# Moving tile starts by small padding tiles, a subtraction from GpSimd to VectorE, and a sixth slot for split weights

## The chip, the cores and the metric

The kernel runs on one core of a Trainium2 chip. The metric is the device time of one execution in microseconds (us); lower is better. TensorE (PE) multiplies, VectorE (DVE), ScalarE (ACT) and GpSimd (POOL) do the element work, and SyncE (SP) issues nearly all loads.

## The reference, cut to what matters

Two transformer blocks follow one another on 256 tokens of width 1024, all in float32. What matters here is where the large products are:

```python
# first block
proj  = rms_norm(x) @ w_in                  # attention, RWKV and memory mixers
x     = x + mixed @ w_out
for e in range(16):                         # mixture of experts, two experts of 16 for each token
    y += gate[:, e:e+1] * ((silu(xt @ w_gate[e]) * (xt @ w_up[e])) @ w_down[e])
x     = x + y
# second block, two layers
h = h + 0.5 * (silu(n(h) @ w1) * (n(h) @ w3)) @ w2     # swiglu, 1024 -> 2816 -> 1024
h = h + mixer(n(h))                                    # layer 0: dilated + top-k attention; layer 1: sliding window
h = h + 0.5 * (silu(n(h) @ w1) * (n(h) @ w3)) @ w2
```

So the second block is, in order: swiglu 0, the hybrid mixer (`hyb`), swiglu 1, swiglu 2, the sliding window mixer (`swa`), swiglu 3.

## The kernel before, in words

**Products in three parts.** A float32 product is made of three matmuls on the type float32r. Each operand is split into a rounded part and what is left (`xh`, `xl` for activations; `wh`, `wl` for weights), and `mm3` (lines 97 to 101) issues rounded x rounded, rounded x rest and rest x rounded into one PSUM bank. In the profile these are the three matmuls of lines 99, 100 and 101. The first operand of a matmul is the stationary one, of 128 columns, loaded by a weight load before it; the second is the moving one, of 256 or 512 columns.

- In `proj2`, `projN` and `project_back` a 128-column slice of the activations (`xh`/`xl`, `hh`/`hl`, `oh`/`ol`, `o`) is stationary, and 512 columns of weights move (256 for the last sixth of a swiglu's gate and up, for `swa_kv` and for `win_m`).
- In `projT` a 128-column slice of the weights is stationary and 256 columns of activations move.
- Parts of the experts' products are plain float32 (lines 1298 and 1324), with 64 stationary columns; they are no part of this.

The profile names a matmul by its operands as out<-moving,stationary: `acc<-wh,xh` has `xh` stationary.

**Splitting the weights.** Weights are loaded in 2 MB pieces into tiles `raw`, and `split` (lines 88 to 95) makes the two parts of 1024 columns at a time: ScalarE rounds (line 93, `wh`), VectorE subtracts (line 94, `wl`). The pair goes into one of five slots in turn, three of the pool `wsp` and two of `lend`, set by the cycle in `weights`. A slot is free again when the last matmul that reads it has run.

**Order.** Each engine's stream is ordered ahead of time by a scheduler that simulates a timeline (`schedule_with_timeline_sim=True`); each engine is then given its stream in that order. So any edit can change the order of neighbours.

**The experts' gather.** In `moe`, `hx` and `hy` are the two parts of the residual `h`. ScalarE rounds (`hx`), GpSimd subtracts (`hy`, line 1171). `gather` (line 1189) multiplies them with 0/1 matrices `P`, which pick 64 tokens for each expert, and the experts follow.

**Where tiles start.** Each partition of the on-chip memory is filled from address 0: first the scratch of `dynamic_dma_scratch_size` bytes, then four constants of 32 bytes each, then the pools in the order in which they are opened, and in a pool one place for each tag and buffer in the order of first use. Sizes are rounded up to 32 bytes. Added up from the shapes, this gives these starts in bytes, and what is left after division by 128 and by 512:

| tile | start before | mod 128 | mod 512 |
|---|---|---|---|
| pool `const` (`ident`, `mhalf`, `cols`, `cm`, `L`, `over`, `flag`) | 1152 | 0 | 128 |
| pool `wk`: `h` | 4544 | 64 | 448 |
| `xh` (also `o` and `yr`) / `xl` (also `o` and `xe`) | 12736 / 20928 | 64 | 448 |
| `raw` (and `memT` in one) | 37760 | 0 | 384 |
| `wh`, `wl` of `wsp` and `lend` | 86912 to 123776 | 0 | 384 |
| experts: `hx`, `hy` and `P` | 162816 to 181248 | 0 | 0 |
| swiglu: `hh` / `hl` | 144256 / 166784 (swiglu 3: 148352 / 170880) | 0 | 384 |
| `hyb`: `oh` / `ol` | 160192 / 168384 | 64 | 448 |
| `swa`: `oh` / `ol` | 149376 / 157568 | 0 | 384 |

Slices of these tiles are 512, 1024 or 2048 bytes apart, so every slice has its tile's rest modulo 512.

Of the kernel before, what the change touches and what calls it, by code (L numbers as in the profile page):

```python
# [11 lines left out]
F32 = mybir.dt.float32  # L12
# [4 lines left out]
OP = mybir.AluOpType  # L17
# [9 lines left out]
class Net:  # L27
# [36 lines left out]
    def setup(self):  # L64
        nc = self.nc
        self.ident = self.const.tile([128, 128], F32, name="ident")
        nc.gpsimd.memset(self.ident, 1.0)
        nc.gpsimd.affine_select(self.ident, self.ident, pattern=[[-1, 128]], compare_op=OP.is_equal,
                                fill=0.0, base=0, channel_multiplier=1)
        self.mhalf = self.const.tile([128, 1], F32, name="mhalf")  # L70
        nc.gpsimd.memset(self.mhalf, -0.5)
        self.cols = self.const.tile([128, NCOL], F32, name="cols")
        nc.scalar.dma_start(self.cols, self.I["cols"])

    def col(self, name, i=0, n=1):
        o = COLS[name][0]
        return self.cols[:, o + i:o + i + n]
# [83 lines left out]
    @contextmanager  # L161
    def weights(self, extra, nsplit):

        with ExitStack() as st:
            pools = list(self.base)
            if extra:
                pools += [st.enter_context(self.tc.tile_pool(name=self.nm("raw"), bufs=extra))] * extra
            self.splits = itertools.cycle([self.wsp] * NW + [self.lend] * nsplit)
            self.ring = itertools.cycle(pools)
            yield  # L170
        self.ring = itertools.cycle(self.base)
# [260 lines left out]
    def hyb(self, h, x, follow):  # L432
        nc, wk = self.nc, self.ph
# [4 lines left out]
                                channel_multiplier=1)  # L438
        xh, xl, rs = x
        ps = self.projN(self.by_k(self.load(self.I["hyb_c"]), 296), 0, 296, xh, xl, True)  # L440
        cw = self.natural(ps, self.pair(264, "cw0", "cw1"), rs)
        kiT = self.repeated_T([z[:, 264:296] for z in ps], rs, "kiT", 1)
        bc = self.row_bc(rs)
        ch = wk.tile([128, 2, T], F32R, name="ch", tag="ch", bufs=1)
# [1 line left out]
        for t in range(2):  # L446
# [3 lines left out]
            ps = self.trp()  # L450
# [680 lines left out]
    def moe(self, h, x):  # L1131

        nc, wk = self.nc, self.ph
        mm, tr, tt = nc.tensor.matmul, nc.tensor.transpose, nc.vector.tensor_tensor
        cm = self.cm
        ck = lambda n: cm[:, COLSM[n][0]:COLSM[n][0] + COLSM[n][1]]
        st = lambda shape, tag, dt=F32: wk.tile([128] + shape, dt, name=self.nm(tag), tag=tag, bufs=1)
        bc = lambda z, *s: z.to_broadcast([128] + list(s))
        L, rs = x
# [7 lines left out]
        for i, op in enumerate((OP.is_ge, OP.is_gt)):  # L1147
# [11 lines left out]
        ps = self.trp()  # L1159
# [7 lines left out]
        hx, hy = ([wk.tile([128, D], F32R, name=self.nm(z), tag=f"{z}{t}", bufs=1) for t in range(2)]  # L1167
                  for z in ("hx", "hy"))
        for t in range(2):
            nc.scalar.copy(hx[t], h[t])  # L1170
            nc.gpsimd.tensor_tensor(hy[t], h[t], hx[t].bitcast(F32), OP.subtract)

        def places(q):

# [260 lines left out]
    def front(self, h):  # L1435

        nc = self.nc
        for t in range(2):
            nc.sync.dma_start(h[t], self.I["x"][t * 128:(t + 1) * 128])
        with ExitStack() as more:  # L1440
            with self.banks(acc=3, tr=2, rk=3), self.weights(0, 0):
                x = self.mixers(h, more, lambda: self.logits(h))
            self.ctx.enter_context(self.banks(acc=6, tr=2))
            with self.phase():
                y = self.moe(h, x)
        ahead = [self.load(self.I["ffn0"][0], 2)]
        self.moe_overflow(h)
        return y, ahead
# [25 lines left out]
NW = 3  # L1474
# [202 lines left out]

# [10 lines left out]
```

## Time and profile before

| | |
|---|---|
| median of 3 runs | 1452.94 us (1452.23 to 1453.97) |
| profiled execution | 1451.34 us, of which the span from first to last instruction is 1449.6 us |
| PE busy / VectorE / ScalarE / GpSimd | 1383.6 / 760.6 / 605.6 / 127.9 us |
| mean granted TensorE clock | 0.983 of 2.4 GHz |

A matmul's duration in the profile overlaps with the next one's, so the time that a matmul costs in a dense stretch is read as the distance between the starts of neighbours, called the pitch below. It is worked out from the first and the last start of a stretch and the number of steps between them.

### The profile page before, as it was taken

To read this page: it belongs to the slowest core of one execution; us is meant where nothing else is said; L and a number is where in the kernel's file an instruction comes from. 1 tells how busy PE (TensorE), PEld (TensorE's weight loads), DVE (VectorE), ACT (ScalarE), POOL (GpSimd) and SP (SyncE) were. 2 spreads that over 40 slices of the span, in tenths; PEclk is the share of its full clock that TensorE was granted. 3 is DMA by queue.
4 is the path that set the end of the run, shared out by engine and by line. 5 is a ranking of instruction groups with operands and counts; after the bars stand their busy time and mean duration, and the time that the engine had idled before them with its cause. 6 is when DMAs were issued, how large, how long until landed. Compare 5 with 4: busy or idle time off the path is not lost.

```text
span 1449.6 us, 18902 instructions
## 1 busy us (share of the span) xinstructions
PE 1383.6 (95%) x7650; PEld 1042.0 (72%) x7650; DVE 760.6 (52%) x1233; ACT 605.6 (42%) x951; POOL 127.9 (9%) x150
## 2 busy tenths in 40 slices
PE   7899989999998999999898999999999989999997
PEld 6687664344336888878677888878888877788886
DVE  6967651112125555456865555455555466555544
ACT  5345431111114444347454444344444456444442
POOL 6514110000001000010111000010000010100001
PEclk9999889999998999999999999999999999999999
DMA  7243379999965544355333544454444632365520
GB/s 305 90 183 139 145 319 368 419 409 419 420 285 213 194 174 175 130 216 194 126 117 139 210 174 174 153 225 175 175 174 160 240 129 111 131 214 182 185 88 29
DMA packets 35371, 293.81 MB, mean 203 GB/s; under 512 B 3728, under 2 KB 8112, under 8 KB 16080
## 3 DMA queue, kind: packets, MB, share of 16 engines
q1 hardware_dynamic: 29952, 286.58, 52.4%
q10 hardware_dynamic: 5328, 5.98, 1.2%
q8 instruction: 62, 1.02, 0.3%
q14 instruction: 29, 0.24, 0.0%
HBM read 291.45 MB, written 1.10 MB: 202 GB/s over the span
## 4 chain that ended last, share of the span: by engine, by line
PE 64%; DVE 2%; ACT 1%; POOL 1%; issue 1%; ACTq 0%; POOLq 0%; DVEq 0%
PE acc L101 20%; PE acc L99 20%; PE acc L100 19%; PE tr L206 1%; PE acc L322 1%; PE tr L318 1%; DVE wl L94 1%; POOL xl L135 1%; ACT wh L93 1%; PE acc L288 1%; PE acc L289 1%; PE acc L323 0%; ACT sq L113 0%; DVE h L371 0%; PE tr L127 0%
## 5 line engine op out<-in xcount | busy, mean ns | idle before, releaser
L94 DVE TENSOR_TENSOR wl<-raw,wh 128x1024 fp32r<-128x1024 f32 (+1 forms) x338 | 412.5, 1223 | 377.6 <-ACT wh L93 377.0
L93 ACT CAST wh<-raw 128x1024 fp32r<-128x1024 f32 (+1 forms) x349 | 363.4, 1045 | 412.8 <-PE acc L101 367.7
L101 PE MATMUL acc<-wh,xl 128*128 128x512 f32 (+2 forms) x896 | 336.0, 376 | 7.2 <-POOL xl L135 7.2
L99 PE MATMUL acc<-wh,xh 128*128 128x512 f32 (+2 forms) x896 | 337.2, 378 | 1.7 <-ACT xh L134 1.2
L100 PE MATMUL acc<-wl,xh 128*128 128x512 f32 (+2 forms) x896 | 335.2, 374 | 3.0 <-DVE wl L94 3.0
L101 PEld LDWEIGHTS acc<-wh,xl 128*128 128x128 f32 x896 | 169.5, 189 | 41.4 <-POOL xl L135 9.2
L100 PEld LDWEIGHTS acc<-wl,xh 128*128 128x128 f32 x896 | 169.8, 190 | 35.3 <-DVE wl L94 3.7
L99 PEld LDWEIGHTS acc<-wh,xh 128*128 128x128 f32 x896 | 169.8, 189 | 35.1 <-ACT xh L134 2.2
L101 PE MATMUL acc<-wh,hl 128*128 128x512 f32 x352 | 137.4, 390 | 0.0
L100 PE MATMUL acc<-wl,hh 128*128 128x512 f32 x352 | 137.2, 390 | 0.0
L99 PE MATMUL acc<-wh,hh 128*128 128x512 f32 x352 | 136.7, 389 | 0.0
L105 POOL TENSOR_SCALAR rstd<-ss 128x1 f32<-128x1 f32 x22 | 8.2, 371 | 940.8 <-ACT sq L113 938.9
L101 PEld LDWEIGHTS acc<-wh,hl 128*128 128x128 f32 x352 | 66.1, 188 | 13.6
L99 PEld LDWEIGHTS acc<-wh,hh 128*128 128x128 f32 x352 | 66.1, 188 | 13.6
L100 PEld LDWEIGHTS acc<-wl,hh 128*128 128x128 f32 x352 | 66.1, 188 | 13.5
L99 PE MATMUL acc<-xh,wh 128*128 128x256 f32 x224 | 65.8, 294 | 2.1 <-DVE cur L653 1.3
L100 PE MATMUL acc<-xl,wh 128*128 128x256 f32 x224 | 63.9, 286 | 1.8 <-POOL xl L135 1.0
L101 PE MATMUL acc<-xh,wl 128*128 128x256 f32 x224 | 64.2, 288 | 0.0
L1298 PE MATMUL acc<-half,xe 128*64 128x512 f32 x248 | 59.6, 596 | 0.0
L1331 DVE TENSOR_SCALAR yf<-tr,gate 128x512 f32<-128x512 f32 x16 | 12.0, 751 | 81.0 <-PE tr L1324 80.8
L99 PEld LDWEIGHTS acc<-xh,wh 128*128 128x128 f32 x224 | 43.4, 194 | 5.9 <-ACT wh L93 2.7
L100 PEld LDWEIGHTS acc<-xl,wh 128*128 128x128 f32 x224 | 43.1, 193 | 2.5 <-POOL xl L135 1.3
(458 smaller groups left out, 1748.7 us busy)
## 6 DMA issues: line engine op xcount, KB each, us to landing
raw<-in_ffn SPq DMA_DIRECT2D x63, 2048.0 KB, 8.0
half<-in_moe SPq DMA_DIRECT2D x45, 1024.0 KB, 12.9
raw<-in_moe SPq DMA_DIRECT2D x13, 2048.0 KB, 15.6
raw<-in_hyb SPq DMA_DIRECT2D x7, 2048.0 KB, 7.9
wl<-in_moe SPq DMA_DIRECT2D x23, 512.0 KB, 13.7
wh<-in_moe SPq DMA_DIRECT2D x23, 512.0 KB, 14.8
raw<-in_win SPq DMA_DIRECT2D x4, 2048.0 KB, 10.1
raw<-in_swa SPq DMA_DIRECT2D x4, 2048.0 KB, 8.7
```

What stands on the lines that cost most here:

```text
L93: nc.scalar.copy(hi[:, :n], x)
L94: self.lo.tensor_tensor(lo[:, :n], x, hi[:, :n].bitcast(F32), OP.subtract)
L99: mm(out, a[0], b[0], start=start, stop=False)
L100: mm(out, a[0], b[1], start=False, stop=False)
L101: mm(out, a[1], b[0], start=False, stop=stop)
L135: (nc.vector if a else nc.gpsimd).tensor_tensor(dl, xf, dh.bitcast(F32), OP.subtract)
L206: nc.tensor.transpose(ps[:, i * 128:(i + 1) * 128], m[:, i * 128:(i + 1) * 128], self.ident)
L288: nc.tensor.matmul(ps[:, 0:128], qT[r, 0:128], kT[r, 0:128], start=True, stop=True)
L289: nc.tensor.matmul(ps[:, 128:384], qT[r, 128:256], kT[r, :], start=True, stop=True)
L318: nc.tensor.transpose(pt[:, i * 128:(i + 1) * 128], s2[e][:, i * 128:(i + 1) * 128], self.ident)
L322: nc.tensor.matmul(po[r, :T], v[0][:, c:c + 64], pT[:, :T], start=True, stop=False)
L1298: last = mm(ps[c][e * 64:e * 64 + 64, :], xe[:, k, o + e * 64:o + e * 64 + 64], w[i][e][:, c * 512:c * 512 + 512], start=k == 0, stop=k == 7)
```

## The change

- `room` makes a tile of a given number of float32 words that nothing reads, and fills it with zeros on GpSimd. One of 16 words (64 bytes) goes into the pool `const` behind `mhalf`, one into the pool `wk` after the experts.
- The scratch shrinks from 1024 to 512 bytes.
- `cw0` and `cw1` of `hyb` take 320 words each where they took 264; the same 264 are used.
- `hy` is made on VectorE, in two halves of 512 columns for each of the two tiles, where GpSimd made each in one.
- Where `weights` is entered for the second block (`nsplit` is 2), the cycle of slots gets a sixth one in a pool of its own.

```diff
         nc.gpsimd.memset(self.mhalf, -0.5)
+        self.room(self.const, 16)
         self.cols = self.const.tile([128, NCOL], F32, name="cols")
...
+    def room(self, pool, words):
+
+        z = pool.tile([128, words], F32, name=self.nm("room"), tag=f"room{words}", bufs=1)
+        self.nc.gpsimd.memset(z, 0.0)
...
-            self.splits = itertools.cycle([self.wsp] * NW + [self.lend] * nsplit)
+            spare = [st.enter_context(self.tc.tile_pool(name=self.nm("spare"), bufs=1))] if nsplit else []
+            self.splits = itertools.cycle([self.wsp] * NW + [self.lend] * nsplit + spare)
...
-        cw = self.natural(ps, self.pair(264, "cw0", "cw1"), rs)
+        cw = self.natural(ps, [z[:, :264] for z in self.pair(320, "cw0", "cw1")], rs)
...
             nc.scalar.copy(hx[t], h[t])
-            nc.gpsimd.tensor_tensor(hy[t], h[t], hx[t].bitcast(F32), OP.subtract)
+            for s in (slice(0, 512), slice(512, 1024)):
+                tt(hy[t][:, s], h[t][:, s], hx[t][:, s].bitcast(F32), OP.subtract)
...
                 y = self.moe(h, x)
+        self.room(self.wk, 16)
         ahead = [self.load(self.I["ffn0"][0], 2)]
...
-    nc = _bacc.Bacc("TRN2", target_bir_lowering=False, num_devices=1, dynamic_dma_scratch_size=1024)
+    nc = _bacc.Bacc("TRN2", target_bir_lowering=False, num_devices=1, dynamic_dma_scratch_size=512)
```

## Rows read from the trace of the kernel before

**Rows 1.** The page's head.
```profile
span 1449.6 us, 18902 instructions
```
**Rows 2.** Busy time of engines by stretch, PE clock and DMA share behind it.
```profile
211.00:440.00 229.00, 222.44 (x1031) 92.52 (x1033) 40.41 (x86) 33.54 (x60) 0.00 (x0) 0.99 0.90 370
452.00:642.00 190.00, 190.00 (x896) 156.81 (x894) 98.67 (x97) 83.14 (x94) 3.08 (x4) 0.99 0.50 181
```
**Rows 3.** Waits of PE in 452 to 1450 us: total, times, longest.
```profile
PE acc L101 <- POOL xl L135: 7.2, 5, 2.2
PE acc L288 <- DVE madd L504: 6.3, 1, 6.3
```
**Rows 4.** Groups by line and shape: count | busy us, mean ns | idle before.
```profile
L94 DVE TENSOR_TENSOR wl<-raw,wh 128x1024 fp32r<-128x1024 f32 x333 | 407.7, 1227 | 374.2 <-ACT wh L93 373.6 <-DVEq L1359 0.2
L99 PE MATMUL acc<-wh,xh 128*128 128x512 f32 x720 | 286.1, 399 | 0.7 <-DVE cur L653 0.3 <-ACT xh L134 0.2 <-ACT lent L413 0.2
L99 PE MATMUL acc<-wh,hh 128*128 128x512 f32 x352 | 136.7, 389 | 0.0
L99 PE MATMUL acc<-xh,wh 128*128 128x256 f32 x224 | 65.8, 294 | 2.1 <-DVE cur L653 1.3 <-ACT wh L93 0.6 <-ACT xh L134 0.2
L99 PE MATMUL acc<-wh,xh 128*128 128x256 f32 x160 | 46.2, 289 | 1.0 <-ACT xh L134 1.0
L1333 DVE TENSOR_TENSOR yr<-yf,yr 128x512 fp32r<-128x512 f32 x16 | 11.0, 690 | 7.2 <-ACT yr L1332 7.1
```
**Rows 5.** Timeline of PE, swiglu 1, gate and up (start us, duration).
```profile
820.02 0.40 PE L99 MATMUL acc<-wh,xh 128*128 128x512 f32 x1
...
825.86 0.39 PE L100 MATMUL acc<-wl,xh 128*128 128x512 f32 x1
```
**Rows 6.** Timeline of PE, swiglu 1, down.
```profile
924.20 0.39 PE L99 MATMUL acc<-wh,hh 128*128 128x512 f32 x1
...
931.00 0.39 PE L99 MATMUL acc<-wh,hh 128*128 128x512 f32 x1
```
**Rows 7.** Timeline of PE, `project_back` of `hyb`.
```profile
767.83 0.39 PE L101 MATMUL acc<-wh,ol 128*128 128x512 f32 x1
...
769.70 0.39 PE L100 MATMUL acc<-wl,oh 128*128 128x512 f32 x1
```
**Rows 8.** Timeline of PE, `project_back` of `swa`.
```profile
1242.01 0.39 PE L101 MATMUL acc<-wh,ol 128*128 128x512 f32 x1
...
1244.28 0.39 PE L99 MATMUL acc<-wh,oh 128*128 128x512 f32 x1
```
**Rows 9.** Timeline of PE, swiglu 1, last sixth of gate and up.
```profile
900.55 0.28 PE L99 MATMUL acc<-wh,xh 128*128 128x256 f32 x1
...
907.24 0.28 PE L101 MATMUL acc<-wh,xl 128*128 128x256 f32 x1
```
**Rows 10.** Timeline of PE, `projT` in `hyb`.
```profile
704.14 0.28 PE L100 MATMUL acc<-xl,wh 128*128 128x256 f32 x1
...
709.55 0.28 PE L101 MATMUL acc<-xh,wl 128*128 128x256 f32 x1
```
**Rows 11.** Timeline of PE, the experts' gather.
```profile
249.24 0.28 PE L1189 MATMUL tr<-P,hy 128*128 128x256 f32 x1
...
250.91 0.28 PE L1189 MATMUL tr<-P,hy 128*128 128x256 f32 x1
```
**Rows 12.** Timeline of all engines before the first gather.
```profile
201.49 2.29 DVE L1229 COPY G<-rstd 128x8 f32<-128x8 f32 x1
...
204.13 2.36 POOL L1171 TENSOR_TENSOR hy<-h,hx 128x1024 fp32r<-128x1024 f32 x1
...
206.44 0.59 POOL L106 TENSOR_TENSOR rstd<-rstd,mhalf 128x1 f32<-128x1 f32 x1
...
209.59 0.17 PE L1160 MATMUL tr<-Mk,count 128*128 128x16 bf16 x1 [2.61 <-DVE o L1206]
```
**Rows 13.** Timeline of VectorE in the top-k of `hyb`.
```profile
697.99 1.21 DVE L94 TENSOR_TENSOR wl<-raw,wh 128x1024 fp32r<-128x1024 f32 x1
```

## The prediction, made before the changed kernel was run

> **What bounds the kernel now.** I read the busy time by stretch first. From 452 to 642 us (swiglu 0) TensorE is busy for all of 190.00 us, VectorE for about half [rows 2]. Then PE's waits: in the whole second block the eight rows of that view add up to 21 us of 1000, of which the two largest stand here: five waits for `xl`, the rest of the activations, at borders between layers (7.2 us), and one stall behind the top-k of `hyb` (6.3 us) [rows 3]. No wait for a split weight (lines 93 and 94) is among them. So the second block takes as long as its matmuls take, and there is one number to look for: the pitch of a matmul, from the starts in the timeline.
>
> The reader is to see that the pitch is not one number for one shape. With 512 moving columns:
>
> - swiglu, gate and up, `xh`/`xl` stationary: 25 steps in 825.86 - 820.02 = 5.84 us, 233.6 ns [rows 5]
> - swiglu, down, `hh`/`hl` stationary: 30 steps in 6.80 us, 226.7 ns [rows 6]
> - `project_back` of `hyb`: 8 steps in 1.87 us, 233.8 ns [rows 7]
> - `project_back` of `swa`: 10 steps in 2.27 us, 227.0 ns [rows 8]
>
> The last two are the same code with the same shapes and order; the weights move from the same slots. They differ in where `oh` and `ol` start: 64 modulo 128 bytes in `hyb`, 0 in `swa`. `xh` and `hh` differ likewise. So a stationary slice that starts at an odd multiple of 64 bytes costs 6.5 to 6.9 ns in each 512-column matmul. The mean durations of the groups show the same sign, 399 against 389 ns [rows 4].
>
> With 256 columns the sign turns: `xh` (64 modulo 128) stationary and `wh` moving takes 59 steps in 6.69 us, 113.4 ns [rows 9]; `wh` (0) stationary and `xh` (64) moving takes 46 steps in 5.41 us, 117.6 ns [rows 10]; `hx`/`hy` and `P`, both at 0 modulo 512, take 14 steps in 1.67 us, 119.3 ns [rows 11].
>
> The Trainium skill (TensorE: Matmul & The Clock Gate, Step-by-step: what each phase is for) says that PE reads the moving and the stationary operand through two independent ports, and that loading the next weights takes nothing from the running matmul. By that rule no start address could matter and the whole sum below would be -1.2 us in place of -12.5. The four pitches above speak against it here.
>
> **The padding, cost by cost.** Adding up the tiles again: the scratch gives back 512 bytes, `room` in `const` adds 64, so `wk` starts at 4544 - 448 = 4096, `xh` and `xl` at 12288 and 20480. `room` in `wk` adds 64, so `raw` starts at 37376, the slots at 86528 and on. After one more `raw` and the sixth slot the layers' pools start at 152064. All of these, `hh`/`hl` and `oh`/`ol` of `swa` too, then leave 0 modulo 512; the 448 bytes in `cw0` and `cw1` bring `oh`/`ol` of `hyb` to 168448, also 0. `hx`, `hy` and `P` go to 128 modulo 512, still 0 modulo 128, and keep the distance between them.
>
> - 512 columns, stationary 64 before, 0 after: in the second block 480 in each of four swiglus (5 x 2 x 16 x 3), 96 in `projN` of `hyb` and 96 in its `project_back`, 2112 together. At 6.5 ns (the pair in which only the start differs): -13.7 us. Bounds: 0, and 6.9 ns x 2112 = 14.6.
> - The same in the mixers of the first block: 144 in three `projN` and 96 in `project_back`, 240 x 6.5 = 1.6 us. There PE also waits for the RWKV chain, so -1.0, between 0 and -1.6.
> - 512 columns with `hh`, or `oh` of `swa`: 0 modulo 128 before and after. I take no change.
> - 256 columns, `xh` stationary: 384 in the swiglus and 48 in `swa_kv`; both operands come to 0 modulo 512, as the gather's are. I take its 119.3 for 113.4 ns: 432 x 5.9 = +2.5 us; if they stay, 0. `win_m` has 48 more: +0.1 beside the first block's other waits.
> - 256 columns, `wh` stationary (`projT`): 672 of them [rows 4], 480 in the second block. 119.3 for 117.6 ns is +0.8 us; if a moving start at 0 brings the 113.4 of the other case, -2.0. I take +0.8.
> - The two fills on GpSimd: in the experts' stretch it does nothing at all [rows 2], and at the start nothing waits for it before the first rows come in. 0.
>
> Sum of the padding: -13.7 - 1.0 + 2.5 + 0.1 + 0.8 = -11.3 us.
>
> **`hy` on VectorE.** Before the first gather GpSimd takes 2.36 us for a half of `hy` from 204.13 on, and the row scale `rstd` of the second 128 tokens stands behind it until 206.44; the routing chain starts from that, and PE waits 2.61 us at 209.59 [rows 12]. Beside the first one a copy of eight columns takes 2.29 us on VectorE, and the copies that PE's router matmuls need are queued behind it. Both go. In their place VectorE has four pieces of 128x512; the nearest row of such a subtraction has 690 ns [rows 4], so 2.8 us; no DMA moves with them. Two of them fit in the time of that copy, the other two while PE does the router's matmuls, which end at about the time at which `rstd` does now; that is the next thing to be late. So the gather starts about 1 us earlier, between 2 us earlier and 0.7 later (one piece in the way). What is won must be kept through the experts, where the DMA engines are busy for 0.90 of the time [rows 2]: a load that has not landed takes some of it back. I take -0.7, from -2.0 to +0.7.
>
> **The sixth slot.** Nothing in the second block waits for a split, so a slot more moves splits earlier and makes none cheaper; VectorE's part of one stays 1.23 us [rows 4]. ScalarE and VectorE still do one for each slot that PE frees. What can change is which split stands in a chain that PE does wait for: one sits in the top-k, 1.21 us [rows 13], and some at the borders between layers. One out of the way is -1.2 us, one more in the way +1.2. I take -0.5, from -3 to +3, which also holds the new order that the scheduler finds.
>
> **Sum.** -11.3 - 0.7 - 0.5 = -12.5 us. The profiled execution takes 1451.34 us (its span is 1449.6 [rows 1]), so 1438.8; it lies 1.6 us under the median of the runs, and for that the sum gives 1452.9 - 12.5 = 1440.4. I predict 1440, with 1434 to 1445 if the terms are right in kind.
>
> **Rivals.**
>
> - *The start address is not the cause* (0.06). Tile and layer differ as well between the pairs, and something else of them might set the pitch. Then only `hy` and the slot are left, -1.2: 1451.7. Against it: four cases, two in one function, sort by the start alone. The Trainium skill (TensorE: Matmul & The Clock Gate, Step-by-step: what each phase is for), by the rule cited above, would have this one.
> - *Round starts help more* (0.12). No 512-column matmul of the trace has its stationary slice at 0 modulo 512; the aligned ones are at 384. 512 columns at 2.4 GHz are 213.3 ns, so 13.4 ns of the 226.7 could still be lost to addresses. If half of that goes in all 3264 of the second block (2112, 1056 of `hh` and 96 of `swa`): -21.9 more, some 1418. Against it: the gather, at 0 modulo 512, has 119.3 - 106.7 (256 columns) = 12.6 ns of the same surplus.
> - *Both operands at 0 modulo 512 collide* (0.06), the slower case. The gather is the only row with this, and it has the largest pitch of its shape, 11.8% over 106.7. If that is a share of the columns and not a constant, 512 columns take 238.5 ns: 2112 x 4.9 + 1152 x 11.8 = +23.9 us in place of the -13.7, some 1478. It decides from a pitch of some 231 ns in all of them, today's mean. Against it: the aligned 512-column cases have 13.4 ns over 213.3, much like the gather's 12.6, so a constant is likelier.
> - *The new order takes some back* (0.14). The padding works and a stall at a border or behind the top-k grows by 4 to 8 us: 1444 to 1449. The 6.3 us stall [rows 3] shows what one such order costs.
>
> **How the numbers follow.** My forecast has 0.62. What cannot be told from no change is 0.2%, 2.9 us. Faster: 0.62 + 0.12 + 0.14 = 0.88; same 0.06 (the first rival); slower 0.06 (the third). The range of 1424 to 1449 holds the forecast, the order rival and a third of the second one; both others and 0.08 of the second lie outside, 0.20.
>
> **What would show each step.** In the profile after: starts 226 to 228 ns apart in gate and up and in `project_back` of `hyb`, and still 227 with `hh`; near 119 ns in the last sixth. Swiglu 1 shorter by 480 x 6.9 ns less 0.5, about 2.8 us. No `hy` on GpSimd, and the first gather's P matmul at about 210 us instead of 211. PE's waits in the second block still near 21 us, with no line 93 or 94 among them. I am wrong if gate and up stay at 233 ns (first rival), if `hh` moves as well (second or third), or if the waits grow by more than 5 us (fourth).

## The result, and the profile after

The changed kernel takes 1440.62 us (median of 4 runs, 1440.14 to 1442.48), the kernel before beside it 1453.03 us (1452.23 to 1453.97): 12.4 us less, ratio 0.9918 (95% interval 0.9906 to 0.9931). The forecast was 1440.

The page's head and the two stretches of [rows 1, 2], now of the changed kernel:

```profile
span 1439.3 us, 18904 instructions
```

```profile
211.00:440.00 229.00, 221.49 (x1025) 92.33 (x1025) 40.93 (x88) 33.55 (x60) 0.00 (x0) 0.99 0.90 371
452.00:642.00 190.00, 188.89 (x894) 158.29 (x895) 97.59 (x98) 84.82 (x99) 5.32 (x8) 0.98 0.50 182
```

PE is nearly as busy as it was (188.89 and 190.00 of 190 us in swiglu 0). The gain is in the pitch. PE's timeline of the changed kernel, with the starts that answer to [rows 5, 6, 7, 9] (its lines 105 to 107 are 99 to 101 of before): gate and up of swiglu 1, its down, `project_back` of `hyb`, and the last sixth.

```profile
816.33 0.39 PE L106 MATMUL acc<-wl,xh 128*128 128x512 f32 x1
...
822.00 0.39 PE L107 MATMUL acc<-wh,xl 128*128 128x512 f32 x1
...
919.19 0.39 PE L107 MATMUL acc<-wh,hl 128*128 128x512 f32 x1
...
925.99 0.39 PE L107 MATMUL acc<-wh,hl 128*128 128x512 f32 x1
...
764.34 0.39 PE L105 MATMUL acc<-wh,oh 128*128 128x512 f32 x1
...
767.97 0.39 PE L107 MATMUL acc<-wh,ol 128*128 128x512 f32 x1
...
895.10 0.28 PE L106 MATMUL acc<-wl,xh 128*128 128x256 f32 x1
...
897.98 0.28 PE L106 MATMUL acc<-wl,xh 128*128 128x256 f32 x1
```

25 steps in 5.67 us, 226.8 ns (233.6 before); 30 steps in 6.80 us, 226.7 ns (226.7); 16 steps in 3.63 us, 226.9 ns (233.8); 24 steps in 2.88 us, 120.0 ns (113.4). Each of these pitches went where the prediction put it.

PE's waits in 452 to 1440 us, the first three rows of that view, beside [rows 3]:

```profile
PE acc L107 <- POOL xl L141: 5.7, 5, 2.2
PE tr L133 <- DVE xf L139: 5.6, 5, 1.6
PE acc L295 <- DVE ka L386: 2.6, 3, 1.7
```

The reader is to see what is not there: the stall of 6.3 us behind the top-k of `hyb`. The prediction did not see it go.

Where the time went, by the first matmul of each stage in the two profiles (us in the stage; the last two columns are runs told of below):

```
stage                     before   after    padding alone   without padding
up to swiglu 0            452.37   454.23   453.66          454.48
swiglu 0                  189.80   189.29   187.19          191.30
hyb                       135.23   130.76   135.16          129.85
swiglu 1                  191.59   190.89   189.11          191.87
swiglu 2                  194.72   191.63   192.30          193.67
swa                        89.02    88.06    88.57           89.10
swiglu 3 and end          196.90   194.49   194.48          197.05
span                     1449.63  1439.35  1440.46         1447.31
```

So 4.5 us come from `hyb`, where the padding's term was 192 x 6.5 = 1.2, the swiglus give 6.7 together, and the first block is 1.9 us longer. Swiglus 0 and 1 give only 0.5 and 0.7 of that. PE's mean granted clock was lower at their starts: 0.87 in the first 20 us of swiglu 0, where it was 0.94 before, and 0.89 in the first 15 us of swiglu 1, where it was 1.00. That is worth some 1.4 and 1.7 us (an estimate: 20 x 0.07 and 15 x 0.11). How much of a single profile is chance is shown by a second profile of the changed kernel (last experiment). The mean clocks of the two:

```profile
core 0: 1439.3 us, clock 0.979
```

```profile
core 0: 1436.7 us, clock 0.984
```

2.6 us lie between two executions of one program, the longer one at the lower granted clock. Single profiles are therefore read here for pitches and waits, and medians for time.

### The profile page after: what moved, and what is told of

Its sections match the earlier page's. It is cut to its first block, busy times and chain, and to the rows that moved or that the text cites. A ratio compares the mean times of both kernels' runs of the same rounds, so it can differ in the third digit from the quotient of the medians.

```text
span 1439.3 us, 18904 instructions
## 1 busy us (share of the span) xinstructions
PE 1379.3 (96%) x7650; PEld 1050.1 (73%) x7650; DVE 757.9 (53%) x1237; ACT 606.4 (42%) x951; POOL 123.0 (9%) x150
## 4 chain that ended last, share of the span: by engine, by line
PE 64%; DVE 2%; ACT 1%; POOL 1%; issue 1%; POOLq 0%; ACTq 0%; DVEq 0%
PE acc L107 20%; PE acc L105 20%; PE acc L106 20%; PE tr L213 1%; PE acc L329 1%; PE tr L325 1%; DVE wl L100 1%; POOL xl L141 1%; PE acc L295 0%; PE acc L296 0%; PE acc L330 0%; ACT sq L119 0%; ACT wh L99 0%; DVE h L378 0%; PE tr L133 0%
## 5 line engine op out<-in xcount | busy, mean ns | idle before, releaser
L105 PE MATMUL acc<-wh,xh 128*128 128x512 f32 (+1 forms) x896 | 335.5, 375 | 2.2 <-ACT xh L140 1.8
L106 PE MATMUL acc<-wl,xh 128*128 128x512 f32 (+1 forms) x896 | 333.7, 373 | 2.3 <-DVE wl L100 2.3
L106 PEld LDWEIGHTS acc<-wl,hh 128*128 128x128 f32 x352 | 66.1, 188 | 13.7
```

What stands on the lines that cost most here:

```text
L105: mm(out, a[0], b[0], start=start, stop=False)
L106: mm(out, a[0], b[1], start=False, stop=False)
```

## Experiments

Three questions: which of the three edits gave the time, whether it is the start of the stationary tile that sets the pitch, and whether there is a better place still. The edits were tried alone, in pairs and all together. In the profiles the padding moves no instruction of PE, VectorE or ScalarE: each padded kernel runs, on these three, the same instructions in the same order as the same kernel without padding. So padding is a change of addresses alone, and the other two edits a change of order (and of the engine of `hy`).

**Padding alone.** The changed kernel less two edits:

```diff
-            for s in (slice(0, 512), slice(512, 1024)):
-                tt(hy[t][:, s], h[t][:, s], hx[t][:, s].bitcast(F32), OP.subtract)
+            nc.gpsimd.tensor_tensor(hy[t], h[t], hx[t].bitcast(F32), OP.subtract)
...
-            spare = [st.enter_context(...)] if nsplit else []
-            self.splits = itertools.cycle([self.wsp] * NW + [self.lend] * nsplit + spare)
+            self.splits = itertools.cycle([self.wsp] * NW + [self.lend] * nsplit)
```

> The padding alone: both fills of 16 words, the smaller scratch and the wider pair of the hyb projection; hy stays on GpSimd and there are five slots. By the prediction's terms the sum is -11.3 us against the kernel before (1441.7 us): gate and up, projN and project_back of hyb at 226 to 228 ns in place of 233, hh as before at 227, 256 columns at 119 to 120. The 6.3 us stall behind the top-k of hyb stays, as the split order is the old one, and the first gather starts at 211 us. Rival: the padding is worth more than that and the other two edits give some of it back; then this kernel beats the changed one, at 1439 or below. Second rival: the gain was that of the new order and not of the addresses; then the time is 1449 us or more.

1443.47 us beside 1453.75, ratio 0.9933 (0.9920 to 0.9945): -9.7 us. Over the whole trace, at full clock, the mean pitch of 512 columns with `xh` goes from 233.3 to 227.3 ns, with `hh` it stays (226.9 and 227.0), 256 columns with `xh` go from 114.2 to 119.8, `projT` from 117.5 to 119.4. The stall in `hyb` stays, here in this kernel's waits of PE:

```profile
PE acc L294 <- DVE madd L510: 6.2, 1, 6.2
```

The first gather is at 212.4 us, not 211. Both rivals fall.

**`hy` on VectorE alone.** Before, with the edit of `hy` from the diff.

> hy on VectorE in four pieces of 128x512 and nothing else; all addresses as before. By the prediction -0.7 us (1452.3), with the first gather at about 210 us. By the trace of the changed kernel, in which two pieces stand ahead of the last copy that the router matmuls need and the gather starts at 211.6 us, it is 0.7 us later here too, and up to 1.9 us is lost until the second block begins: 1453.5 to 1455. Third: the loss of the changed kernel's first block comes from elsewhere, and this one is at 1453.0 with a gather at 211.0.

1455.71 us, ratio 1.0008 (0.9999 to 1.0017): +1.2 us, not clear of no change, and no gain. Its first gather is at 211.6 us.

**The sixth slot alone.** Before, with `spare` from the diff.

> The sixth slot alone; tiles behind the slots move by its size, which is a multiple of 128 bytes, so no start modulo 128 changes. By the prediction -0.5 us (1452.5). Rival: the slot is what took the wait of 6.3 us behind the top-k of hyb out of the changed kernel (2.6 us stand there in its place); then PE's waits in the second block fall by about 3.7 us and the time is some 1449.3. Second rival: that wait went with the padding, as the scheduler orders anew; then the stall stays at about 6 us and the time at 1453.

1454.40 us, ratio 1.0007 (0.9998 to 1.0016): +1.0 us, not clear of no change either. The stall is there, 6.3 us. Neither the slot nor the padding alone took it away.

**The stationary start or the distance.** Before, with the first fill and the smaller scratch only:

```diff
+        self.room(self.const, 16)
         self.cols = self.const.tile([128, NCOL], F32, name="cols")
...
-    nc = _bacc.Bacc("TRN2", target_bir_lowering=False, num_devices=1, dynamic_dma_scratch_size=1024)
+    nc = _bacc.Bacc("TRN2", target_bir_lowering=False, num_devices=1, dynamic_dma_scratch_size=512)
```

> Before with the fill of 16 words in const and the smaller scratch only. So xh and xl start at 0 modulo 128 bytes, but the slots of the split weights (wh, wl) and hh, hl at 64, oh of hyb at 0, oh of swa at 64. It tells the start of the stationary tile from the distance between the two operands. If the stationary start alone sets the pitch: gate and up 227 ns with the moving weights at 64, project_back of hyb 227, hh and project_back of swa 233, xh with 256 columns 120, projT (now wh at 64 stationary) 113 in place of 118. In us: 2112 x -6.5 = -13.7, 1152 x 6.5 = +7.5, 432 x 5.9 = +2.5, 480 x -4.2 = -2.0, mixers -1.0: -6.7, 1446.3. If it is the distance (both at the same offset modulo 128 or not): gate and up stay at 233, hh at 227 (both at 64), no change, 1453. If the moving start counts as well: gate and up between these, 230 ns.

1452.75 us, ratio 0.9993 (0.9985 to 1.0002): no change. PE's timeline in swiglu 1, gate and up (`xh` at 0, `wh` at 64) and down (`hh` and `wh` at 64):

```profile
816.20 0.39 PE L106 MATMUL acc<-wl,xh 128*128 128x512 f32 x1
...
822.03 0.39 PE L107 MATMUL acc<-wh,xl 128*128 128x512 f32 x1
...
925.40 0.39 PE L107 MATMUL acc<-wh,hl 128*128 128x512 f32 x1
...
932.20 0.39 PE L107 MATMUL acc<-wh,hl 128*128 128x512 f32 x1
```

25 steps in 5.83 us, 233.2 ns, with a round stationary start (0 modulo 128); 30 steps in 6.80 us, 226.7 ns, with an odd one (64). `project_back` of `hyb` (`oh` at 0) has a mean of 233.4, that of `swa` (at 64) 228.5. It is the distance between the two operands, not the start of one. The prediction had the cause wrong; before and after could not tell, since the weights lie at 0 modulo 128 in both.

**The pairs.** Padding and slot:

> The changed kernel with hy back on GpSimd: padding and sixth slot. Each engine but GpSimd (two fills more) has the instruction order of the run with the slot alone, so only addresses differ between the two. If addresses and order add up: 10.3 us under the slot alone (1454.4), that is some 1444, with the 6.3 us wait behind the top-k of hyb there as it was with the slot alone. By the prediction's terms (hy -0.7): 1441.3. If the slot gives more once the padding is there: 1440 and no such wait.

1444.77 us beside 1453.62, ratio 0.9938 (0.9924 to 0.9952): -9.0 us, with a stall of 6.2 us.

Padding and `hy`:

> The changed kernel without the sixth slot: padding and hy on VectorE. It has the order of the run with hy alone. If addresses and order add up: 10.3 us under that (1455.7), some 1445, with the wait of 6.3 us behind the top-k. By the prediction's terms (slot -0.5): 1441.1. If hy gives more once the padding is there: 1440.

1444.09 us, ratio 0.9939 (0.9925 to 0.9952): -8.9 us, with a stall of 6.2 us.

`hy` and slot, without padding:

> The changed kernel without the padding: hy on VectorE and the sixth slot at the addresses of before. It has the order of the changed kernel on TensorE, VectorE, ScalarE and SyncE, and no other run has that one: the top-k of hyb is taken apart, with attention work between its steps on VectorE. If the order of these two edits together takes the wait of 6.3 us away, it shows 2 to 3 us there and takes some 1451 (1440.6 + 10.3), 2.5 under before, though each edit alone was about 1 us over it. If the two edits add up as they did alone: 1456. By the prediction's terms: 1452.5.

1449.02 us, ratio 0.9970 (0.9958 to 0.9981): -4.4 us, where the two alone were at +1.2 and +1.0. Its waits of PE in `hyb` begin with

```profile
PE acc L289 <- DVE ka L380: 2.9, 4, 1.8
```

The long stall is gone at the old addresses. The reason stands in the order of VectorE's stream. First the kernel with padding alone, VectorE in the top-k, then the changed kernel:

```profile
698.81 0.28 DVE L508 MATCH_REPLACE8 rep<-m,rep 128x128 f32<-128x128 f32 x1
699.00 0.41 DVE L385 SCALAR_TENSOR_TENSOR ka<-acc,bc 128x256 f32<-128x256 f32 x1
699.34 0.21 DVE L510 TENSOR_SCALAR madd<-rep 128x128 f32<-128x128 f32 x1
```

```profile
696.68 0.27 DVE L509 MATCH_REPLACE8 rep<-m,rep 128x128 f32<-128x128 f32 x1
696.87 0.41 DVE L386 SCALAR_TENSOR_TENSOR ka<-acc,bc 128x256 f32<-128x256 f32 x1
697.20 0.28 DVE L507 MAX8 m<-rep 128x8 f32<-128x128 f32 x1
```

and the matmul of PE that reads `ka`, in the same two kernels:

```profile
699.57 0.81 PE L294 MATMUL acc<-ka,qa 64*128 64x128 f32 x4 [6.23 <-DVE madd L510]
```

```profile
697.43 0.50 PE L295 MATMUL acc<-ka,qa 64*128 64x128 f32 x4 [1.74 <-DVE ka L386]
```

`ka` is what PE needs next. With padding alone it is queued behind the whole first top-k (`madd`, which the waits name, is only the instruction after it). With the order that `hy` and the slot have together, it stands after the second of the eight steps, and PE waits 1.7 us in place of 6.2.

The stall also goes with a lower clock: the same four matmuls take 0.81 us behind the long wait and 0.50 behind the short one. All engines in 690 to 710 us, in the kernel before and in `hy` and slot without padding (PE's granted clock is the third number from the end):

```profile
690.00:710.00 20.00, 13.66 (x106) 12.14 (x105) 18.96 (x71) 6.64 (x16) 2.26 (x3) 0.83 0.19 80
690.00:710.00 20.00, 17.89 (x150) 15.53 (x146) 19.89 (x70) 11.22 (x25) 0.24 (x1) 1.00 0.35 121
```

In the seven profiles with the long wait it is 0.83, in the seven without 0.91 or 1.00. `hyb` is 5.4 us shorter without padding than before (135.23 to 129.85). PE's waits behind VectorE in the top-k give 3.9 of that (6.3 and 0.5 to 2.9); what the clock gives of the other 1.5 is not shown by itself.

**Is there a better place?** The changed kernel, with the split weights of 256-column products moved 64 bytes on in their slots. That takes splits of three k in place of four, where a k is the 256 columns of one 128-row block of the weights:

```diff
-    def split(self, x):
+    def split(self, x, skew=0):
...
-        hi, lo = (p.tile([128, 1024], F32, name=self.nm(z), tag=z).bitcast(F32R) for z in ("wh", "wl"))
+        hi, lo = (p.tile([128, 1024], F32, name=self.nm(z), tag=z).bitcast(F32R)[:, skew:skew + n] for z in ("wh", "wl"))
...
-        kk = 1024 // ncol
-        parts = [self.split(w[:, i * 1024:(i + 1) * 1024]) for i in range(8 * ncol // 1024)]
+        kk, skew = (3, 16) if ncol == 256 else (1024 // ncol, 0)
+        parts = [self.split(w[:, i * ncol:min(i + kk, 8) * ncol], skew) for i in range(0, 8, kk)]
```

> The changed kernel with the split weights of the last sixth of each swiglu and of swa_kv 64 bytes further on in their slot, and for that in pieces of three k (768, 768 and 512 columns in place of two of 1024). So with 512 columns both operands start at the same offset modulo 128, and with 256 columns and xh stationary they lie 64 apart. If the distance decides: 113 to 114 ns in place of 120 for 432 matmuls of the second block, -2.7 us, some 1438, below both kernels. If the stationary start decides (0 in both): 120 ns and no gain. The extra splits cost nothing if TensorE waits for none of them; if it does, up to 10 x 1.2 us.

1441.25 us, ratio 0.9915 (0.9901 to 0.9929): the changed kernel's time. The pitch is 118, neither 113 nor 120. Then the distances in steps, with a fill of its own ahead of each swiglu's `hh` and a skew for each:

```diff
+        self.skew = SKEW[idx]
+        if ROOM[idx]:
+            self.room(self.ph, ROOM[idx])
...
-        self.room(self.wk, 16)
+        self.room(self.wk, 32)
...
+SKEW = (32, 48, 64, 80)
+ROOM = (32, 48, 64, 80)
```

> Here every swiglu has another distance, by which the moving slice starts behind the stationary one. The runs so far show it as the distance that counts, with its sign (modulo 512 bytes): at 0, 227 ns with 512 columns and 120 with 256; at -64, 233 and 113; at +64, 118 with 256. In this kernel the fill in wk has 32 words (xh against wh at +64 with 512 columns), each swiglu has a fill ahead of hh (hh against wh at -128, -192, -256, -320 in swiglu 0 to 3), and its last sixth is moved in its slot (256 columns at +192, +256, +320, +384). If only zero or not modulo 128 counts: 227 at -128 and -256, 233 at -192, -320 and for xh. If the period is 512: other values can turn up; 512 columns below 226 ns, or 256 below 113, would be a better place than the changed kernel's. If the distance plays no part: 227 and 120 everywhere. Time: 10 us over the changed kernel if xh is at 233, else near it.

The second has a fill of 48 words in `wk`, `SKEW = (80, 88, 96, 112)` and `ROOM = (96, 112, 8, 128)`.

> The same with other distances: fill in wk of 48 words (xh against wh at +128 with 512 columns); hh against wh at -384, -448, -32, -512 in swiglu 0 to 3; 256 columns at +448, +480, +512, +576. If the period is 512: hh in swiglu 3 at 227 as at 0, hh in swiglu 1 as xh in the run before (+64), 256 columns at +448 as at -64 (113), at +512 120, at +576 118. If only zero or not modulo 128 counts: xh and hh in swiglu 0 at 227, and 256 columns at +448 and +576 alike. Time: with xh at 227 that of the changed kernel, 1441.

One run each: 1447.38 and 1454.10 us, beside 1453.76. In the first, PE's timeline with `xh` at +64, then `hh` at -128 (swiglu 0), -256 (swiglu 2) and -320 (swiglu 3):

```profile
460.27 0.40 PE L105 MATMUL acc<-wh,xh 128*128 128x512 f32 x1
...
464.86 0.39 PE L106 MATMUL acc<-wl,xh 128*128 128x512 f32 x1
...
590.05 0.39 PE L107 MATMUL acc<-wh,hl 128*128 128x512 f32 x1
...
594.93 0.39 PE L107 MATMUL acc<-wh,hl 128*128 128x512 f32 x1
...
1101.80 0.39 PE L105 MATMUL acc<-wh,hh 128*128 128x512 f32 x1
...
1104.98 0.39 PE L107 MATMUL acc<-wh,hl 128*128 128x512 f32 x1
...
1382.63 0.39 PE L105 MATMUL acc<-wh,hh 128*128 128x512 f32 x1
...
1384.96 0.39 PE L106 MATMUL acc<-wl,hh 128*128 128x512 f32 x1
```

20 steps at 229.5 ns, 21 at 232.4, 14 at 227.1 and 10 at 233.0. The mean of all starts at full clock, over before, after and these runs, by the start of the moving slice less that of the stationary one modulo 256 bytes:

```
distance   512 columns (ns)   256 columns, xh stationary (ns)
0          226.9 to 227.4     119.8
64         229.1 to 229.4     117.8 to 117.9; 114.4 in one place
128        232.3 to 232.5     118.5 to 118.6
192        233.3 to 233.4     113.8 to 114.5; 117.6 in two places
224        233.3              118.4
```

With 512 columns the pitch repeats after 256 bytes: -256 and -512 have 227, as 0, and -192 and -448 have 229, as +64. At 128 it is 232, so 128 bytes is not a period. 0 is the best place; before was at 192, the worst with 224. With 256 columns the distance does not settle it.

**The skew at 448 bytes, beside the changed kernel.** `(3, 112)` in place of `(3, 16)`.

> The kernel of the run with the skewed last sixth, with 448 bytes in place of 64: 512 columns stay at distance 0 (227 ns, the best place that any run showed), 256 columns with xh stationary in the swiglus and in swa_kv come to +448, which had 113 to 114 ns in swiglu 0 of the run before. 432 matmuls by 6 ns: -2.6 us against the changed kernel (beside it on the same chip), some 1438. If the 113 belonged to that one layer and not to the place: 118 ns, -0.8 us.

> The changed kernel as it is, beside the one above on the same chip, so that a difference of 2 to 3 us can be told: 1440 to 1442.

1441.99 us (1440.82 to 1442.69) and 1440.24 us (1438.41 to 1442.89; ratio to before 0.9911, 0.9897 to 0.9925): no gain. In the last sixth of swiglu 0 this kernel and the second of the distance runs have the same operands at the same addresses. Their timelines of PE there:

```profile
573.25 0.28 PE L106 MATMUL acc<-wl,xh 128*128 128x256 f32 x1
...
576.91 0.28 PE L107 MATMUL acc<-wh,xl 128*128 128x256 f32 x1
```

```profile
575.01 0.28 PE L106 MATMUL acc<-wl,xh 128*128 128x256 f32 x1
...
578.99 0.28 PE L105 MATMUL acc<-wh,xh 128*128 128x256 f32 x1
```

31 steps at 118.1 ns and 35 at 113.7. So the second value that was expected came: the 113 does not belong to the place. What else sets it stays open. By stage the skew gives 0.2 us in each of swiglus 2 and 3, and `swa` is 1.8 us longer than in the first profile of the changed kernel, in the new order that the extra pieces bring.

## Why the prediction was right

The total was right, by terms that were not. In us against before (ratio by 1453.7), each interval some 1.3 to 2 us to either side:

```
                        old order   hy      slot    hy and slot
old addresses           0           +1.2    +1.0    -4.4
padding                 -9.7        -8.9    -9.0    -11.9 and -12.9
```

1. **The padding, -11.3 forecast: -9.7 alone; -10.1, -10.0 and -7.5 to -8.5 in the other orders.** Right in kind, every pitch as forecast, and a little too large. The mis-sized term is that of 512 columns with the stationary slice at 64. Its 6.5 ns were said to be those of the two `project_back`, but these lie 233.8 - 227.0 = 6.8 ns apart [rows 7, 8]. Over the whole trace it is 233.3 - 227.3 = 6.0 ns, so 2112 x 6.0 = 12.7 in place of 13.7 us. With the measured +2.4 (432 x 5.6) and +0.9 (480 x 1.9) for 256 columns that makes -9.4, and with -1.0 for the mixers, which no run measured by itself, -10.4. Swiglus 2 and 3 show it bare: 129.43 to 127.09 and 128.80 to 126.45 us from the first gate to the first down matmul. For swiglu 1 some 2.8 were forecast: 129.95 to 127.47 with padding alone, but only to 128.98 in the changed kernel, where the clock was lower.
2. **Its cause.** The step that failed: "a stationary slice that starts at an odd multiple of 64 bytes costs 6.5 to 6.9 ns". It is the distance of the two operands modulo 256 bytes. The sum held because in before and after the weights lie at a round start, so the stationary start was the distance. A padding that moved the slots along would have been forecast as a gain and given none, which is the run with the first fill alone: -6.7 by the stationary start, measured -1.0 (-2.2 to +0.3).
3. **The Trainium skill.** Its rule of two independent ports (TensorE: Matmul & The Clock Gate, Step-by-step: what each phase is for), as the first rival read it, would have left the time at 1451.7. The trace disagrees with that reading: 227 to 233 ns for one instruction, by the distance of the two operands.
4. **`hy`, -0.7 forecast (-2.0 to +0.7): +1.2 alone (-0.1 to +2.5).** The first gather is at 211.6 us, not 210. The part that was right: `rstd` of the second half is ready at 203.7 in place of 207.0. The part that failed is what is late next. VectorE and PE in the changed kernel, beside [rows 12]:

```profile
203.96 1.28 DVE L1179 TENSOR_TENSOR hy<-h,hx 128x512 fp32r<-128x512 f32 x2
205.16 0.68 DVE L1129 COPY hT<-tr 128x512 f32<-128x512 f32 x1
...
207.83 0.24 DVE L1135 SCALAR_TENSOR_TENSOR L<-acc,rstd,cm 128x20 f32<-128x20 f32 x1 [1.99 <-PE acc L1133]
```

```profile
205.90 1.90 PE L1133 MATMUL acc<-rg,hT 128*128 128x20 f32 x8 [0.18 <-DVE hT L1129]
```

Two pieces were put ahead of the last `hT` copy, which PE's router matmuls need, and those end at 207.8 (eight in 1.90 us; before, sixteen took 2.57). The mean granted clock in 203 to 211 us was 0.54, before 0.66. "One piece in the way" was the forecast's worst end; here two were, with a lower clock on top. Over the fourteen profiles the first gather is at 210.8 to 212.5 us, with `hy` on either engine.
5. **The slot, -0.5 forecast (-3 to +3, with the new order): +1.0 alone (-0.3 to +2.3), and with `hy` together -4.4, or -2.2 to -3.2 on the padding.** No wait for a split went, as forecast. What was mis-sized is the order. The fourth rival named the top-k stall as the price of an unlucky order; here the order was a lucky one: PE's wait at that place fell from 6.3 to 1.8 us, and the clock behind it was no longer as low. It needs both edits; why the scheduler finds this order only with both stays open.
6. **Rivals.** The start address is not the cause: the start of one operand is not, as the run with the first fill shows, but moving the tiles did change the pitch. Round starts help more: no, `hh` stays at 227 at 384 modulo 512 and at 0, and no distance was below 227. Both at 0 collide: no, 0 is the best place with 512 columns; with 256 it is the worst, as the gather's row said.

So -11.3 - 0.7 - 0.5 stands against about -9.7 and -2 to -3: the luck of the order made up for what the padding and `hy` fell short.

## What to carry to other kernels

If one shape of matmul shows two pitches in one trace, compare where its two operands start, both of them, before settling on one; then move one tile by a few words, which leaves the order of instructions alone and so can be measured by itself. Edits that let a scheduler order anew should be tried alone and together: two that gained nothing alone won 4.4 us together, and the trace shows one instruction that moved ahead of a long chain. A forecast that comes out right to 1 us can still hold a wrong cause, and only an experiment that puts the causes apart shows it.

## What the runs showed of the hardware

- The pitch of a float32r matmul with 512 moving columns at full clock depends on the start of its moving slice less that of the stationary slice modulo 256 bytes: 227 ns at 0, 229 at 64, 232.4 at 128, 233.3 at 192 and at 224.
- With 256 columns it is 120 ns at 0, and at 64 and 192 one of two values, near 114 or near 118; the same addresses gave both in two kernels. Open.
- In the seven profiles in which PE waits 6.2 to 6.5 us behind the top-k of `hyb`, its mean granted clock in 690 to 710 us is 0.83; in the seven without that wait it is 0.91 or 1.00.
- Two executions of one program differ by 2.6 us in span, 1439.3 and 1436.7, at mean granted clocks of 0.979 and 0.984.
